# Early results fetched one slice ahead, final transposes in the small banks, and weight sums on VectorE, in a macaron FFN block

## The chip, the cores and the metric

The kernel runs on one core of a Trainium2 chip. Its time is that of one launch, in device microseconds (us). TensorE has two clock levels, 1.2 and 2.4 GHz; the profile gives the granted clock as a share of the upper one.

## The reference

One layer of a streaming encoder on x of 1024 tokens by 1024 features, all in fp32: a half-step FFN, a mixing stage (a chunkwise matrix-memory branch and a spatial gating branch), a second half-step FFN and a final norm.

```python
def swiglu(x, w_in, w_out):
    gate, up = jnp.split(x @ w_in, 2, axis=-1)
    return (jax.nn.silu(gate) * up) @ w_out
...
        x = x + 0.5 * swiglu(rmsnorm(x, ffn1_norm_g[l]), ffn1_w_in[l], ffn1_w_out[l])
        xn = rmsnorm(x, mix_norm_g[l])
        proj = xn @ w_mix_in[l]
...
        x = x + merged @ w_mix_out[l]
        x = x + 0.5 * swiglu(rmsnorm(x, ffn2_norm_g[l]), ffn2_w_in[l], ffn2_w_out[l])
    return rmsnorm(x, final_norm_g)
```

The hidden width `D_FF` is 2816, which is 22 slices of 128 columns. Only the two FFNs and the final norm are touched here.

## The kernel before

**Numbers and products.** Every fp32 operand is split into a high part (a cast on ScalarE, engine name ACT) and a low part (a subtract on VectorE, DVE), both fp32r. A product takes three matmuls (high by high, high by low, low by high), so four contraction tiles are 12 matmuls of 128x512. `unit` makes such a pair of a weight tile into the pool `fw` of four buffers, `split` does it for activations.

**The input GEMM of an FFN** is done by a Strassen-like scheme over a 2x2 partition: gate and up columns by the halves of the contraction, and the two halves of the tokens. Of the seven products of a slice, two depend on the token half whose operand is there first. `first_products` makes them for all 22 slices at the start of the FFN and stores the two results per slice (a partial sum, and a silu) in DRAM, tiles `eb`. `group(f)` does the rest of slice f, in this order:

- four loads of raw weights into two tiles of the pool `raw` (four buffers; L284, issued by SyncE, SP), then the two early results `p1` (L329) and `sg1` (L331) from `eb` into temporaries `c`, on the same queue;
- ScalarE copies `p1` into a PSUM bank x (L333), which opens the accumulation there;
- GpSimd (POOL) makes three sums of weight tiles (`sums`, L303 to L305): s1 = a21 + a22, a21 = a11 - a21, a11 = s1 - a11. Since they work in place, each waits for the raw tiles of both halves;
- five products of 12 matmuls (L297): t2 into x, t1 into a bank b, t3 into y (y is a copy of x, L338), 22 into x, t4 into y. The operands of t1, t3 and 22 are sums; that of 22 is one more subtract on GpSimd, L348. VectorE adds and multiplies what comes out (L347, L351, L355, L356) and makes the operands of the output GEMM (L367 to L373, L196).

**The output GEMM.** Slices are worked in blocks of 4, 4, 4, 4, 2 and 4. Each of the first four blocks has its output GEMM in `down_fast`, 4 x 42 matmuls, whose weight sums (L303 to L305 with 128x256 operands) are made by VectorE already and whose results are added into DRAM by DMAs on GpSimd's queue. A block's output GEMM is written behind the first slice of the next block, so the slice that follows it is the second of that block (slices 5, 9, 13, 17). Block 5 (slices 16 and 17) uses `down` behind slice 18. The last block, slices 18 to 21, uses `last`: for each of 8 output tiles d, 12 matmuls (L444), an add of the residual on VectorE (L471), and in the second FFN `fin2`, which transposes the sum on TensorE (L1021), multiplies it by the norm's gain (L1024) and, when the row's statistic is there, scales it (L1038).

**Buffers and order.** PSUM has 8 banks; in both FFNs seven are `mm`, from which `bank("mm")` takes, and one is `ml`, from which `psm()` takes for statistics and small things. The temporaries `c` and `t512` share 11 buffers. The program is written by hand; a scheduler at build time then fixes the order on each engine, and each engine and each DMA queue works its own list strictly in that order.

Of the kernel before, what the change touches and what calls it, by code (L numbers as in the profile page):

```python
# [11 lines left out]
ALU = mybir.AluOpType  # L12
# [7 lines left out]
NF = DFF // P  # L20
# [14 lines left out]
def block_body(ctx, tc, x, ffn1_norm_g, ffn1_w_in, ffn1_w_out, mix_norm_g, w_mix_in, mlstm_conv_w,  # L35
               mlstm_conv_b, mlstm_b_igate, mlstm_b_fgate, mlstm_head_norm_g, sgu_norm_g, sgu_norm_b,
               sgu_w_s, sgu_b_s, w_mix_out, ffn2_norm_g, ffn2_w_in, ffn2_w_out, final_norm_g, out):
    nc = tc.nc
    V, A, PE, G = nc.vector, nc.scalar, nc.tensor, nc.gpsimd
    x = x[0]  # L40
    out = out[0]
# [8 lines left out]
    def open_psum(stack, n, **bufs):  # L50
        for tag, b in bufs.items():
            psum[tag] = stack.enter_context(
                tc.tile_pool(name=f"{tag}{n}", bufs=b, space=bass.MemoryType.PSUM, reuse_waits="tile"))

    def bank(tag):
        return psum[tag].tile([P, NH], F32, tag=tag, name=tag)

    f1 = ExitStack()
# [3 lines left out]
    def open_temps(stack, n, bufs):  # L62
        raws.append(stack.enter_context(tc.tile_pool(name=f"rawp{n}", bufs=3 if n == 2 else 4, reuse_waits="tile")))
        tps.append(stack.enter_context(tc.tile_pool(name=f"tp{n}", bufs=bufs, reuse_waits="tile")))

    open_temps(f1, 1, TMP)
    open_psum(f1, 1, mm=7, ml=1)

    def t512():
        return tps[-1].tile([P, NH], F32, tag="t512", name="t512")  # L70
# [1 line left out]
    def psm():  # L72
        return bank("ml")
# [42 lines left out]
    def pc(nm, i):  # L116
        return par[:, col[nm] + i:col[nm] + i + 1]
# [29 lines left out]
    def spread():  # L147
        if todo:
            todo.pop(0)()
# [115 lines left out]
    def evens(src):  # L265
        return src[:, :, 0, :], src[:, :, 1, :]

    class Ffn:
# [39 lines left out]
        def first_products(self, fs):  # L308
# [9 lines left out]
            for f, a, e in st:  # L318
# [2 lines left out]
                A.activation(out=e[:, 1, :], in_=a, func=AF.Silu)  # L321
                G.dma_start(out=self.eb[f][1], in_=e[:, 1, :])

        def group(self, f):
            r1, r2 = self.raw(f, 0, True), self.raw(f, 1, True)
            a11, a21 = evens(r1)
            a12, a22 = evens(r2)
            p1 = self.c512()
            nc.sync.dma_start(out=p1, in_=self.eb[f][0])  # L329
            sg1 = self.c512()  # L330
            nc.sync.dma_start(out=sg1, in_=self.eb[f][1])  # L331
            x = bank("mm")
            A.copy(out=x, in_=p1)  # L333
            s1 = self.sums(G, a11, a12, a21, a22, 4)
            w = self.unit(a11)
            self.prod(x, w, self.B["t2"], False, True)
            y = bank("mm")
            A.copy(out=y, in_=x)  # L338
            w = self.unit(s1)
            b = bank("mm")  # L340
            self.prod(b, w, self.B["t1"], True, True)
            p5 = self.c512()
            A.copy(out=p5, in_=b)
            w = self.unit(a21)
            self.prod(y, w, self.B["t3"], False, True)
            c22 = self.c512()
            V.tensor_tensor(out=c22, in0=y, in1=p5, op=ALU.add)  # L347
            G.tensor_tensor(out=a12, in0=a12, in1=a11, op=ALU.subtract)  # L348
            w = self.unit(a12)
            self.prod(x, w, self.B["22"], False, True)  # L350
            V.tensor_tensor(out=p5, in0=x, in1=p5, op=ALU.add)  # L351
            A.activation(out=p5, in_=p5, func=AF.Silu)
            w = self.unit(a22)
            self.prod(y, w, self.B["t4"], False, True)
            V.scalar_tensor_tensor(out=sg1, in0=y, scalar=0.5, in1=sg1, op0=ALU.mult, op1=ALU.mult)  # L355
            V.scalar_tensor_tensor(out=c22, in0=c22, scalar=0.5, in1=p5, op0=ALU.mult, op1=ALU.mult)  # L356
            u3 = sg1
            if f >= FAST:
                self.hs.append((self.part(self.hp, u3), self.part(bigp, c22)))
            elif f % 2 == 0:  # L360
                self.H["11"].append(self.part(self.hp, u3))
                self.odd = u3, c22
            else:
                h11, h12 = self.odd
                H = self.H
                H["21"].append(self.part(self.hp, u3))
                V.tensor_tensor(out=h11, in0=h12, in1=h11, op=ALU.subtract)  # L367
                H["t1"].append(self.part(bigp, h11))
                V.tensor_tensor(out=h12, in0=c22, in1=h12, op=ALU.subtract)
                H["t3"].append(self.part(bigp, h12))  # L370
                V.tensor_tensor(out=h11, in0=c22, in1=h11, op=ALU.subtract)
                H["t2"].append(self.part(bigp, h11))
                V.tensor_tensor(out=u3, in0=u3, in1=h11, op=ALU.subtract)  # L373
                H["22"].append(self.part(self.hp, c22))
                H["t4"].append(self.part(bigp, u3))
# [99 lines left out]

        def run(self, src, final, parts, hook):
            pend = None
            for bi, (f0, n) in enumerate(BLOCKS):
                hs = self.hs = []
                H = self.H = {k: [] for k in ("11", "21", "22", "t1", "t2", "t3", "t4")}  # L480
                for f in range(f0, f0 + n):
                    self.group(f)
                    if pend is not None:
                        pend()
                        pend = None
                    spread()
                if f0 < FAST:
                    pend = lambda f0=f0, H=H: self.down_fast(f0, H, src)
                elif bi < len(BLOCKS) - 1:
                    pend = lambda f0=f0, n=n, hs=hs: self.down(f0, n, hs, src)  # L490
                else:
                    self.last(f0, n, hs, src, final, parts, hook)
# [488 lines left out]
        xn2, bcs, st = mix(mx, xnm)  # L981

    with ExitStack() as f2:
        open_psum(f2, 3, mm=7, ml=1)
        open_temps(f2, 3, TMP)
        ffn2 = Ffn(f2, "2", ffn2_w_in[0], ffn2_w_out[0])
        ffn2.B["11"], ffn2.B["21"] = xn2[:4], xn2[4:]

        def get2(j, i, t):
            b = ffn2.c512()  # L990
            d = 4 * j + i
            if t == 0:
                G.dma_start(out=b, in_=xs_[1][d])
                return b
            G.dma_start(out=b, in_=xd[1][t][d])
            V.scalar_tensor_tensor(out=b, in0=b, scalar=pc("g2", d), in1=bcs[t], op0=ALU.mult, op1=ALU.mult)
            return b

        ffn2.first_products((0, 1))
        bcs.append(st.bcast())  # L1000
        for i in range(4):
            ffn2.first_products((2 * i + 2, 2 * i + 3))
            ffn2.operands(i, get2)
        for f in range(10, NF, 2):
            ffn2.first_products((f, f + 1))

        PARTS = (1, 2)
        sts = [[Stats(4 // p) for _ in range(p)] for p in PARTS]
        fgs = []
        ys = []  # L1010

        def fin2(h, d, part, xt):
            n = 4 // PARTS[h]
            if not fgs:
                fgs.append(bigp.tile([P, D], F32, tag="big", name="fg"))
                nc.sync.dma_start(out=fgs[0], in_=final_norm_g.partition_broadcast(P))
            fg = fgs[0]
            sts[h][part].add(xt)
            ps = bank("mm")
            for t in range(n):  # L1020
                PE.transpose(out=ps[:, t * P:(t + 1) * P], in_=xt[:, t * P:(t + 1) * P], identity=ident)  # L1021
            if d % 2 == 0:
                ys.append(bigp.tile([P, n, 2 * P], F32, tag="big", name="y"))
            V.tensor_tensor(out=ys[-1][:, :, (d % 2) * P:(d % 2 + 1) * P],  # L1024
                            in0=ps[:, 0:n * P].rearrange("p (t c) -> p t c", c=P),
                            in1=fg[:, None, d * P:(d + 1) * P].to_broadcast([P, n, P]), op=ALU.mult)
            if d < KT - 1:
                return
            r = sts[h][part].rstd()
            t0 = h * NH + part * n * P  # L1030
            ov = out[t0:t0 + n * P, :].rearrange("(t p) c -> p t c", p=P)
            for i in range(4):
                y = ys.pop(0)
                for t in range(n):
                    if t == n - 1:
                        A.activation(out=y[:, t, :], in_=y[:, t, :], func=AF.Copy, scale=r[:, t:t + 1])  # L1036
                    else:
                        V.tensor_scalar(out=y[:, t, :], in0=y[:, t, :], scalar1=r[:, t:t + 1], scalar2=None,  # L1038
                                        op0=ALU.mult)
                nc.sync.dma_start(out=ov[:, :, i * 2 * P:(i + 1) * 2 * P], in_=y)  # L1040

        ffn2.run(xd[1], fin2, PARTS, lambda t, xs: None)


# [25 lines left out]
```

## Time and profile before

| | before |
|---|---|
| median of 3 runs | 2380.12 us (2379.06 to 2381.86) |
| the profiled execution, its own time | 2376.19 us |
| its span in the trace | 2374.4 us |
| mean granted clock | 0.979 |
| TensorE busy | 2258.1 us, 95% |
| VectorE busy | 1453.2 us, 61% |
| ScalarE busy | 1120.8 us, 47% |
| GpSimd busy | 496.7 us, 21% |

The span runs from the first to the last record of one execution; its own time is 1.8 us more. Matmul is PE in the rows, weight load PEld. TensorE stands for some 5% of the span, and part of its busy time is at a clock below the upper level.

### The profile page before, as it was taken

Reading aid. Unit: us, or ns where it says so; the run is one execution under the profiler, and the core shown is the slowest. Engines: PE = TensorE matmul, PEld = TensorE weight load, DVE = VectorE, ACT = ScalarE, POOL = GpSimd, SP = SyncE. Lnnn points to the kernel's source line nnn. Section 1 sums busy time; section 2 is a strip of 40 time slices with the busy share of each in tenths; the row PEclk is TensorE's granted clock in tenths of the full one; section 3 lists DMA queues with packets and bytes.
Section 4 is the critical chain, followed back from the end, with each engine's and each line's share of the span. In section 5 each row is a group of like instructions: output and inputs, shape, how many; then the busy total and the mean of one; then the engine's idle time right before and its main releaser. Section 6 shows DMA issues by size and latency. Waiting matters only on the chain. (4 is left out here: it accounts for less than half of the span.)

```text
span 2374.4 us, 30679 instructions
## 1 busy us (share of the span) xinstructions
PE 2258.1 (95%) x10979; PEld 1881.8 (79%) x10979; DVE 1453.2 (61%) x2563; ACT 1120.8 (47%) x1924; POOL 496.7 (21%) x557
## 2 busy tenths in 40 slices
PE   7999999999899999999999999999999999999896
PEld 5888787777778988888889878887887787777675
DVE  6647676675366757656656666564647576765355
ACT  5545454444444356444445455453545454544432
POOL 3242433414520000000000000001241524324420
PEclk8999999999999999999999999999999999999999
DMA  8853655637753334233343433325762745646632
GB/s 271 252 179 98 142 117 132 133 89 138 155 186 109 88 85 135 83 89 89 115 129 93 134 113 93 92 83 178 247 190 89 151 108 132 129 120 133 147 110 89
DMA packets 331512, 311.51 MB, mean 131 GB/s; under 512 B 19160, under 2 KB 279896, under 8 KB 331360
## 3 DMA queue, kind: packets, MB, share of 16 engines
q1 hardware_dynamic: 292608, 217.20, 31.1%
q0 software_dynamic: 38752, 92.36, 17.8%
q8 instruction: 86, 1.41, 0.2%
q14 instruction: 66, 0.54, 0.1%
HBM read 223.48 MB, written 86.02 MB: 130 GB/s over the span
## 5 line engine op out<-in xcount | busy, mean ns | idle before, releaser
L297 PE MATMUL mm<-b,fw 128*128 128x512 f32 x2640 | 626.4, 399 | 56.7 <-ACT mm L333 55.7
L297 PEld LDWEIGHTS mm<-b,fw 128*128 128x128 f32 x2640 | 508.1, 193 | 174.6 <-ACT mm L333 64.0
L291 DVE TENSOR_TENSOR fw<-raw,fw 128x512 fp32r<-128x512 f32 (+1 forms) x472 | 316.0, 676 | 396.4 <-ACT fw L290 394.9
L162 PE MATMUL mm<-xn,w 128*128 128x512 f32 x2304 | 546.6, 391 | 0.0
L162 PEld LDWEIGHTS mm<-xn,w 128*128 128x128 f32 x2304 | 427.0, 188 | 82.8
L297 PE MATMUL mm<-h,fw 128*128 128x512 f32 x1344 | 313.6, 393 | 5.8 <-ACT fw L290 3.1
L297 PEld LDWEIGHTS mm<-h,fw 128*128 128x128 f32 x1344 | 248.5, 188 | 69.6 <-ACT fw L290 8.2
L290 ACT CAST fw<-raw 128x512 fp32r<-128x512 f32 (+1 forms) x472 | 247.8, 526 | 101.5 <-PE mm L297 71.6
L138 DVE TENSOR_TENSOR w<-raw,w 128x1024 fp32r<-128x1024 f32 (+3 forms) x160 | 178.6, 1117 | 163.6 <-ACT w L137 163.2
L297 PE MATMUL mm<-xn,fw 128*128 128x512 f32 x1056 | 247.4, 396 | 3.6 <-ACT xn L195 2.1
L297 PEld LDWEIGHTS mm<-xn,fw 128*128 128x128 f32 x1056 | 200.5, 191 | 49.4 <-ACT xn L195 3.7
L137 ACT CAST w<-raw 128x1024 fp32r<-128x1024 f32 (+3 forms) x160 | 153.8, 963 | 178.7 <-PE mm L162 86.2
L176 PE MATMUL mm<-w,xn 128*128 128x256 f32 x1344 | 163.9, 282 | 0.0
L176 PEld LDWEIGHTS mm<-w,xn 128*128 128x128 f32 x1344 | 161.8, 189 | 1.4 <-issue 0.5
L256 POOL DMA_DIRECT2D xs<-t x16 | 8.6, 541 | 642.0 <-DVE t L253 641.3
L195 ACT CAST h<-c 128x512 fp32r<-128x512 f32 x136 | 82.2, 621 | 69.1 <-DVE c L355 26.3
L303 POOL TENSOR_TENSOR s<-raw 128x512 f32<-128x512 f32 x44 | 59.4, 1351 | 205.7 <-DMA raw<-in_ffn_w_in_dram 190.3
L444 PE MATMUL mm<-h,wl 128*128 128x512 f32 (+1 forms) x480 | 97.3, 356 | 0.3 <-DVE h L196 0.2
L196 DVE TENSOR_TENSOR h<-c,h 128x512 fp32r<-128x512 f32 x136 | 91.1, 689 | 5.9 <-ACT h L195 4.8
L409 POOL DMA_DIRECT2D xd<-c x32 | 28.0, 874 | 309.6 <-ACT fw L290 273.0
L444 PEld LDWEIGHTS mm<-h,wl 128*128 128x128 f32 x480 | 78.4, 192 | 12.5 <-DVE h L196 0.7
L162 PE MATMUL po<-mh,w 128*128 128x512 f32 x384 | 87.5, 389 | 0.0
(258 smaller groups left out, 2607.6 us busy)
## 6 DMA issues: line engine op xcount, KB each, us to landing
raw<-in_ffn_w_in_dram SPq DMA_DIRECT2D x264, 256.0 KB, 3.4
raw<-in_w_mix_in_dram SPq DMA_DIRECT2D x96, 512.0 KB, 3.8
xd<-c POOLq DMA_DIRECT2D x160, 256.0 KB, 5.2
eb<-early POOLq DMA_DIRECT2D x88, 256.0 KB, 2.8
c<-eb SPq DMA_DIRECT2D x88, 256.0 KB, 4.3
raw<-in_ffn_w_out_dram SPq DMA_DIRECT2D x72, 256.0 KB, 3.0
raw<-in_w_mix_in_dram SPq DMA_DIRECT2D x32, 384.0 KB, 3.4
xl<-xd POOLq DMA_DIRECT2D x32, 256.0 KB, 4.4
```

Of the source, the lines that this page charges most:

```text
L137: A.copy(out=w[:, 0, 0:n, :], in_=raw[:, 0:n, :])
L138: V.tensor_tensor(out=w[:, 1, 0:n, :], in0=raw[:, 0:n, :], in1=w[:, 0, 0:n, :].bitcast(F32), op=ALU.subtract)
L162: PE.matmul(out=banks[j], lhsT=w[:, a, i, j * P:(j + 1) * P], rhs=act[k][:, b, ts], start=(k == first and pi == 0), stop=(k == last and pi ...
L176: PE.matmul(out=o, lhsT=act[k][:, b, t * P:(t + 1) * P], rhs=w[:, a, i, :], start=(t % 2 == 0 and k == 0 and pi == 0), stop=(t % 2 == 1 an ...
L195: A.copy(out=dst[:, 0, :], in_=src)
L196: V.tensor_tensor(out=dst[:, 1, :], in0=src, in1=dst[:, 0, :].bitcast(F32), op=ALU.subtract)
L290: A.copy(out=w[:, 0], in_=src)
L291: V.tensor_tensor(out=w[:, 1], in0=src, in1=w[:, 0].bitcast(F32), op=ALU.subtract)
L297: PE.matmul(out=bank, lhsT=w[:, x, i, :], rhs=t[:, y, :], start=(start and i == 0 and pi == 0), stop=(stop and i == len(b) - 1 and pi == 2 ...
L303: G.tensor_tensor(out=s1, in0=a21, in1=a22, op=ALU.add)
L409: G.dma_start(out=acc[0][d], in_=c11, accum_op=ALU.add)
L444: PE.matmul(out=o, lhsT=w[:, x, i, :], rhs=hs[i][:, y, ts], start=(i == 0 and pi == 0), stop=(i == n - 1 and pi == 2))
```

## The change

Three edits. `group(f)` no longer loads its own early results; a new `fetch(f + 1)` is written right behind slice f's raw loads, and `fetch(0)` at the start of `run`. In both FFNs the PSUM split goes from 7 and 1 to 6 and 2, and the final transposes take `psm()`. The three sums of `group` and the subtract of a12 go from GpSimd to VectorE: 4 operations for each of 22 slices in two FFNs, 176 in all.

```diff
-    open_psum(f1, 1, mm=7, ml=1)
+    open_psum(f1, 1, mm=6, ml=2)
...
+        def fetch(self, f):
+            self.ahead = self.c512(), self.c512()
+            for t, src in zip(self.ahead, self.eb[f]):
+                nc.sync.dma_start(out=t, in_=src)
+
         def group(self, f):
             r1, r2 = self.raw(f, 0, True), self.raw(f, 1, True)
             a11, a21 = evens(r1)
             a12, a22 = evens(r2)
-            p1 = self.c512()
-            nc.sync.dma_start(out=p1, in_=self.eb[f][0])
-            sg1 = self.c512()
-            nc.sync.dma_start(out=sg1, in_=self.eb[f][1])
+            p1, sg1 = self.ahead
+            if f + 1 < NF:
+                self.fetch(f + 1)
             x = bank("mm")
             A.copy(out=x, in_=p1)
-            s1 = self.sums(G, a11, a12, a21, a22, 4)
+            s1 = self.sums(V, a11, a12, a21, a22, 4)
...
-            G.tensor_tensor(out=a12, in0=a12, in1=a11, op=ALU.subtract)
+            V.tensor_tensor(out=a12, in0=a12, in1=a11, op=ALU.subtract)
...
             pend = None
+            self.fetch(0)
...
-        open_psum(f2, 3, mm=7, ml=1)
+        open_psum(f2, 3, mm=6, ml=2)
...
-            ps = bank("mm")
+            ps = psm()
```

Lines of `group` from L333 on stand four lines lower afterwards (L337, L342, L351, L352 for the subtract, L355, L359, L360), L444 is L448, L1021 is L1026. How the built lists differ is seen at three places.

**SyncE's queue, first FFN, around slice 9**, the first slice behind an output GEMM. `eb080` and `eb081` are slice 8's early results, `eb090` and `eb091` slice 9's, `eb0100` and `eb0101` slice 10's; `raw_3328` and `raw_3331` (before) are slice 9's weights, `raw_3453` and `raw_3456` slice 10's. Before:

```order
L386 DMA raw_3058<-in_ffn1_w_out_dram 128x4x128 x2
L329 DMA c_2868<-eb080_197 128x512
L331 DMA c_2870<-eb081_198 128x512
L386 DMA raw_3148<-in_ffn1_w_out_dram 128x4x128 x2
L386 DMA raw_3238<-in_ffn1_w_out_dram 128x4x128 x2
L284 DMA raw_3328<-in_ffn1_w_in_dram 128x4x128 x2
L284 DMA raw_3331<-in_ffn1_w_in_dram 128x4x128 x2
L284 DMA raw_3453<-in_ffn1_w_in_dram 128x4x128 x2
L284 DMA raw_3456<-in_ffn1_w_in_dram 128x4x128 x2
L329 DMA c_3334<-eb090_199 128x512
L331 DMA c_3336<-eb091_200 128x512
```

After:

```order
L390 DMA raw_3062<-in_ffn1_w_out_dram 128x4x128 x2
L327 DMA c_2872<-eb090_199 128x512
L327 DMA c_2873<-eb091_200 128x512
L390 DMA raw_3152<-in_ffn1_w_out_dram 128x4x128 x2
L390 DMA raw_3242<-in_ffn1_w_out_dram 128x4x128 x2
L284 DMA raw_3332<-in_ffn1_w_in_dram 128x4x128 x2
L284 DMA raw_3335<-in_ffn1_w_in_dram 128x4x128 x2
L284 DMA raw_3457<-in_ffn1_w_in_dram 128x4x128 x2
L284 DMA raw_3460<-in_ffn1_w_in_dram 128x4x128 x2
L327 DMA c_3338<-eb0100_201 128x512
L327 DMA c_3339<-eb0101_202 128x512
```

The places in the list are the same; what stands at each is the pair of the next slice. Slice 9's pair is now ahead of two tiles of `w_out` and of four raw tiles, its own and slice 10's.

**VectorE, same place.** `c_3377` and `c_3394` (before) are slice 9's p5 and c22, `raw_3453` and `s_3465` slice 10's weights and sum. Before, from slice 9's last weight units on:

```order
L291 TENSOR_TENSOR fw_3414<-raw_3331,fw_3414 128x512
L291 TENSOR_TENSOR fw_3469<-raw_3453,fw_3469 128x512
L347 TENSOR_TENSOR c_3394<-mm_3359,c_3377 128x512
L291 TENSOR_TENSOR fw_3486<-s_3465,fw_3486 128x512
L351 TENSOR_TENSOR c_3377<-mm_3338,c_3377 128x512
L291 TENSOR_TENSOR fw_3504<-raw_3453,fw_3504 128x512
```

After, where `raw_3457` and `raw_3460` are slice 10's weights, `raw_3563` and `raw_3566` slice 11's, `c_3381` and `c_3398` slice 9's p5 and c22:

```order
L291 TENSOR_TENSOR fw_3418<-raw_3335,fw_3418 128x512
L291 TENSOR_TENSOR fw_3473<-raw_3457,fw_3473 128x512
L303 TENSOR_TENSOR s_3575<-raw_3563,raw_3566 128x512
L351 TENSOR_TENSOR c_3398<-mm_3363,c_3381 128x512
L291 TENSOR_TENSOR fw_3490<-s_3469,fw_3490 128x512
L304 TENSOR_TENSOR raw_3563<-raw_3563 128x4x128
L305 TENSOR_TENSOR raw_3563<-s_3575,raw_3563 128x4x128
L355 TENSOR_TENSOR c_3381<-mm_3342,c_3381 128x512
L291 TENSOR_TENSOR fw_3508<-raw_3457,fw_3508 128x512
L352 TENSOR_TENSOR raw_3566<-raw_3566,raw_3563 128x4x128
```

The first sum of slice 11, which needs slice 11's raw tiles, stands ahead of slice 9's c22 and of slice 10's second weight unit, and three more new operations stand between the rest.

**TensorE, the end of the program**, the first output tiles of the last output GEMM. Before:

```order
L444 MATMUL mm<-h,wl 128x512 x12
L1021 MATMUL mm<-ident,xl 128x128 x4
L444 MATMUL mm<-h,wl 128x512 x12
L1021 MATMUL mm<-ident,xl 128x128 x4
L444 MATMUL mm<-h,wl 128x512 x12
```

After:

```order
L448 MATMUL mm<-h,wl 128x512 x19
L1026 MATMUL ml<-ident,xl 128x128 x4
L448 MATMUL mm<-h,wl 128x512 x9
L1026 MATMUL ml<-ident,xl 128x128 x4
L448 MATMUL mm<-h,wl 128x512 x12
```

The transposes of a tile stood directly behind its own 12 matmuls; now 7 of the next tile's 12 matmuls stand between at first, 4 from the second tile on, and 8 and more where the tiles are 256 wide.

## Rows read from the trace of the kernel before

**Rows 1.** The page's busy times and its header.
```profile
span 2374.4 us, 30679 instructions
...
PE 2258.1 (95%) x10979; PEld 1881.8 (79%) x10979; DVE 1453.2 (61%) x2563; ACT 1120.8 (47%) x1924; POOL 496.7 (21%) x557
```

**Rows 2.** TensorE's waits: total us, times, longest.
```profile
PE mm L297 <- ACT mm L333: 55.7, 18, 9.6
PE mm L1021 <- DVE xl L471: 16.8, 23, 3.2
```

**Rows 3.** What line L333 waits for, and L329's issue to landing.
```profile
  DMA c<-eb: 115.3, 40
...
DMA to landing us min/median/max: 3.0/4.2/8.4
```

**Rows 4.** Timeline around slice 9: start us, us; in brackets idle before, releaser.
```profile
359.74 0.44 SPq L329 DMA_DIRECT2D c<-eb  x1
...
363.00 12.22 SPq L284 DMA_DIRECT2D raw<-in_ffn_w_in_dram  x4
...
366.44 0.59 ACT L333 COPY mm<-c 128x512 f32<-128x512 f32 x1 [2.41 <-DMA c<-eb]
...
367.08 3.36 PE L297 MATMUL mm<-b,fw 128*128 128x512 f32 x7 [4.19 <-ACT mm L333]
...
375.32 0.45 SPq L329 DMA_DIRECT2D c<-eb  x1
```

**Rows 5.** Windows after the ten longest L333 waits: us, PE busy, clock, DMA.
```profile
265.03:275.03 10.00, 10.00 (x37) 0.83 0.67 154
...
2243.99:2253.99 10.00, 10.00 (x33) 0.73 0.59 117
sum 100.00, PE 99.99; mean PE 10.00
```

**Rows 6.** Chain that ended last, the first tile pair of the tail.
```profile
2290.42 0.75 PE mm L444 x2
2291.19 0.70 DVE xl L471
...
2291.94 0.66 PE mm L1021 x4
```

**Rows 7.** Two slices without a wait: PE, PEld, DVE, ACT, POOL, clock.
```profile
397.60:424.90 27.30, 27.30 (x120) 22.63 (x121) 23.11 (x38) 13.86 (x26) 4.14 (x3) 1.00 0.33 97
```

**Rows 8.** Lines of GpSimd's sums and VectorE's like operations: busy, mean ns, idle before.
```profile
L305 POOL TENSOR_TENSOR raw<-s,raw 128x512 f32<-128x512 f32 x44 | 74.2, 1687 | 1.7
L348 POOL TENSOR_TENSOR raw<-raw 128x512 f32<-128x512 f32 x44 | 67.3, 1530 | 3.1
L304 POOL TENSOR_TENSOR raw<-raw 128x512 f32<-128x512 f32 x44 | 64.2, 1459 | 2.0
L303 POOL TENSOR_TENSOR s<-raw 128x512 f32<-128x512 f32 x44 | 59.4, 1351 | 205.7 <-DMA raw<-in_ffn_w_in_dram 190.3 <-DVE c L347 13.9 <-DVE fw L291 1.4
...
L356 DVE SCALAR_TENSOR_TENSOR c<-c 128x512 f32<-128x512 f32 x44 | 51.9, 1180 | 5.3 <-ACT c L352 5.0
...
L367 DVE TENSOR_TENSOR c<-c 128x512 f32<-128x512 f32 x16 | 11.1, 692 | 0.6
```

**Rows 9.** VectorE's timeline, two operations back to back.
```profile
388.67 0.68 DVE L373 TENSOR_TENSOR c<-c 128x512 f32<-128x512 f32 x1
389.27 0.68 DVE L196 TENSOR_TENSOR h<-c,h 128x512 fp32r<-128x512 f32 x1
```

**Rows 10.** Timeline: slice 9's c22 and slice 11's first sum.
```profile
377.92 0.69 DVE L347 TENSOR_TENSOR c<-mm,c 128x512 f32<-128x512 f32 x1 [0.89 <-PE mm L297]
...
378.98 1.43 POOL L303 TENSOR_TENSOR s<-raw 128x512 f32<-128x512 f32 x1 [9.31 <-DMA raw<-in_ffn_w_in_dram]
```

**Rows 11.** Timeline: slice 20's first sum, slice 19's first product.
```profile
626.45 1.25 POOL L303 TENSOR_TENSOR s<-raw 128x512 f32<-128x512 f32 x1 [6.78 <-DMA raw<-in_ffn_w_in_dram]
...
631.07 17.26 PE L297 MATMUL mm<-b,fw 128*128 128x512 f32 x67 [6.99 <-ACT mm L333]
```

## Prediction

> **What bounds the kernel now.** I read the busy times first: TensorE is at work for 2258.1 of 2374.4 us [rows 1]. The reader is to see that no engine beside it is near the span, so the time is matmuls, the time TensorE stands, and the time it works at the lower clock. The second view is therefore the list of TensorE's waits, since only a wait there is sure to be on the path. One entry leads it: 55.7 us in 18 waits for the copy at L333, which puts slice f's early result into its bank; next come 16.8 us in 23 waits of the final transposes for the add at L471 [rows 2]. The third view is what L333 itself waits for: DMAs out of `eb`, 115.3 us in 40 waits, although a load lands some 4.2 us after its issue [rows 3]. So the load is issued late, and the timeline says why: slice 9's pair stands on SyncE's queue behind slice 10's raw loads (the order shows it), is issued at 359.74, its copy runs at 366.44, and TensorE starts at 367.08 after 4.19 us of nothing; slice 11's raw loads then hold the queue for 12.22 us, and slice 10's pair goes at 375.32 [rows 4].
>
> The fourth view is windows of 10 us behind the ten longest of these waits. They show what a wait costs beyond itself: the granted clock there is 0.83, 0.75, 0.77, 0.83, 0.81, 0.69, 0.85, 0.83, 0.74 and 0.73 [rows 5], though TensorE is busy throughout. Behind waits under 2 us it stays at 1.00, as in the two slices of [rows 7]. A window at clock c does 10c us of full-speed work, so the loss is 10 times the sum of (1 - c): 10 x (10 - 7.83) = 21.7 us.
>
> **Early results a slice ahead.** The two orders of SyncE's queue show that places stay and contents move by one slice. Slice 9's pair takes the place of slice 8's, some 52 us earlier (four output tiles of 42 matmuls at 0.2275 us, the 27.30/120 of [rows 7], and a slice of 13.65); slice 10's pair goes at 359.74 where slice 9's went, lands by 366.4, and is wanted when slice 9 is done: TensorE would start slice 9 at 367.08 - 4.19 = 362.9, and end it at 376.5. There are 10 us to spare. No DMA is added: 88 pairs' halves before, 88 after. The loads ahead on the queue take a `c` buffer each, two of eleven, which then are out of use for a slice longer; a load that waited for a buffer would hold the raw loads behind it. The buffers they reuse come from temporaries of a slice or an output tile earlier, so I cost that at nothing; its cover is the same 10 us, and if it is gone the raw loads are late by the rest. **Gain: 55.7 + 21.7 = 77.4 us.** The low end is 55.7, if something else lowers the clock there. What is late next at these places is the weight unit, and I come to it below.
>
> **Final transposes in the small banks.** TensorE's order at the end shows what decides: before, a tile's four transposes stand directly behind its own 12 matmuls and wait for the residual's add, as in the chain: matmuls end at 2291.17, the add takes 0.70, the transposes start at 2291.94 [rows 6]. Afterwards some of the next tile's matmuls stand between, 4 at the least with 512 columns (0.91 us at 0.2275) and 8 or more with 256. That covers an add of 0.70 and the way to it. **Gain: 16.8 us**; the last tile keeps its wait, under a microsecond. With one bank for transposes instead of several, the multiply at L1024 would hold the next transposes; there are two, and a tile's 12 matmuls lie between two uses. The input GEMM has six banks for seven. A slice takes three, x, y and b, so two slices in flight fit. I cost it at nothing: the first writer of a bank waits, at the worst, for a read of the bank three places earlier. If that cover is gone, each slice pays one copy of 0.59 [rows 4], 44 x 0.59 = 26 us.
>
> **Sums on VectorE.** 176 operations go off GpSimd, where they take 59.4 + 64.2 + 74.2 + 67.3 = 265 us [rows 8], off the path: no TensorE wait names them. On VectorE the like operation is L367, fp32 from two SBUF tiles, 692 ns [rows 8]; back to back such operations start 0.60 us apart [rows 9]. In two steady slices VectorE ran 38 records in a window of 27.30 us [rows 7]; by the program a pair has 29 operations (10 in an even slice, 19 in an odd one), which become 37. At 0.605 that is 22.4 us in 27.3, so VectorE keeps up, with 4.9 us a pair to spare, and I cost the work itself at nothing. It gets a little back: L356 takes 1180 ns beside GpSimd's L348 and should fall towards 700 when GpSimd is quiet.
>
> By the Trainium skill, page "VectorE: DVE Perf Modes", section "The DRAIN you can't avoid", the next operation does not start until the pipe is empty, unless it is one that is not held back. Taken as it stands each would cost its whole 0.69, and a pair 37 x 0.69 = 25.5 us of 27.3; [rows 9] show a start 0.60 after the last one, so the trace does not agree for such neighbours, and the sum goes by the row.
>
> The same skill's page "Perfetto Trace Analysis", section "Optimizing Scalar/DVE Operations", says that GpSimd and VectorE share a read port, so that moving work between the two might not help. By that alone the 176 operations would bring VectorE 1.35 to 1.69 us each; [rows 8] have 692 ns for L367, and nothing of GpSimd's adds is left to share with.
>
> What does cost is the wait that comes along. The order puts slice f+2's first sum ahead of slice f's c22 and of the second unit of slice f+1 on VectorE. That sum needs f+2's raw tiles, and GpSimd has waited for them until now, 190.3 us in 34 waits [rows 8], where it hurt nobody. In steady slices VectorE comes to it when c22 could run, at 377.92, and the tiles are there for the sum at 378.98 [rows 10]: 1.1 us in which c22 and the units behind it stand. Later units have some 1 to 2 us of lead by my count of 37 x 0.605, less at the end of a block. I take 0.5 us of TensorE for each of the eight blocks with a fast output GEMM, 4 us. Slice 19 is worse: slice 20's tiles are there at 626.45 [rows 11], and slice 19, freed of its 6.99 us wait, would start at 631.07 - 6.99 = 624.1 and want its t1 unit one product later, at 626.8; three sums and a subtract behind the landing it is ready at 626.45 + 4 x 0.605 = 628.9. That is 2 us in each FFN, 4 us. **Loss: 8 us**; its bounds are nothing, and 1.5 us in each of 32 slices with the clock's loss on top, about 60.
>
> **Sum.** 2376.2 (the profiled execution's own time) - 77.4 - 16.8 + 8 = 2290.0. That execution was 3.9 us under the median of the runs shown; as the terms are absolute, the median should be 2380.1 - 86.2 = 2293.9. I predict 2294.
>
> **The rivals.**
> - Forecast, chance 0.70: some 86 us less, 2280 to 2308.
> - VectorE's waits for raw tiles come through to TensorE, 0.15. For it speaks that its list is strictly in order and the new sums wait for DMAs; against it that the tiles land about when c22 is wanted. At 1.5 us in each of the 32 slices of the fast blocks, 48 us, and a lower clock behind a few of them, some 10, it is 2294 - 8 + 58 = 2344. Still faster.
> - VectorE becomes the bound, 0.07, the one on the other side. Its place is the pair of slices; it decides when waits at the head of its list exceed the 1.7 us (37 operations at L367's 0.692 are 25.6) to 4.9 us (at 0.605) a pair that are over. If each of two sums a pair waits as long as slice 9 did for its raw loads, 6.1 us (half of the 12.22 us issue of [rows 4]), a pair takes 25.6 + 12.2 = 37.8 instead of 27.3. Over 16 pairs that is 168 us, and 2380 - 94 + 168 = 2454. Against it: raw loads are issued when buffers come free, so a slower TensorE has them in time, and the loop does not feed itself.
> - The fetch does not do what it says, 0.05: its place on the queue is again behind loads that wait, and the pair is as late as before. Then the transposes alone count: 2380 - 17 = 2363. The two lists speak against it.
> - The sums cost what the rest gains, 0.03: no change.
>
> **How the numbers follow.** The first case alone goes from 2280 (no loss on VectorE and a few short waits gone too) to 2308 (twice the loss, half the clock's gain kept). For 8 in 10 the range reaches part of the way to the second: 2274 to 2335. A measurement of this kernel can tell about 0.2%, 4.8 us, from no change. Faster: 0.70 + 0.15 + 0.05 less a little of each = 0.88; same 0.04; slower 0.08.
>
> **What would show it.** Right: TensorE's waits for the copy of the early result (L337) under 5 us; the clock near 1.00 behind each output GEMM; the waits of the transposes (L1026) under 2 us; the four sums gone from GpSimd, on VectorE at about 0.69 us with waits of 1 to 2 us for raw tiles ahead of the first. Wrong: TensorE waits named after the weight subtract (L291) or cast (L290) of tens of microseconds, or for bank releases in the copies (L342). The prediction fails if VectorE's waits reach TensorE in every slice, or if the clock falls at other places for them.

## The result

The changed kernel takes 2304.06 us (median of 4 runs, 2298.88 to 2308.23) where the kernel before, run beside it, takes 2380.99 (2379.06 to 2382.28): a ratio of 0.9676, 95% interval 0.9655 to 0.9698. That is 76.9 us less; 86 were forecast, and 2304 lies in the stated range. The profiled execution of the changed kernel took 2305.36 us.

The header and the busy times of its page, which answer to [rows 1]:

```profile
span 2303.6 us, 30578 instructions
...
PE 2231.6 (97%) x10979; PEld 1872.1 (81%) x10979; DVE 1466.3 (64%) x2739; ACT 1119.3 (49%) x1924; POOL 252.7 (11%) x381
```

176 operations have left GpSimd and are on VectorE, whose busy time rose by only 13 us. TensorE's waits in the changed kernel, answering to [rows 2] (total us, times, longest):

```profile
PE mm L297 <- DVE fw L291: 17.8, 2, 11.0
PE mm L297 <- DVE c L351: 17.1, 9, 2.8
...
PE ml L1026 <- DVE xl L475: 0.5, 1, 0.5
```

Neither wait that the change aimed at is left: no entry names the copy of the early result (L337), and the transposes wait 0.5 us in all. Two new entries of 34.9 us stand in their place, where the prediction had 8. Both come from the sums' waits, which now stand on VectorE:

```profile
DVE s L303 <- DMA raw<-in_ffn_w_in_dram: 101.1, 39, 17.6
```

The larger price is at slice 19 of each FFN. The changed kernel's timeline there (start, us, idle before and its releaser in brackets):

```profile
605.82 0.69 DVE L303 TENSOR_TENSOR s<-raw 128x512 f32<-128x512 f32 x1 [17.62 <-DMA raw<-in_ffn_w_in_dram]
606.54 0.69 DVE L304 TENSOR_TENSOR raw<-raw 128x512 f32<-128x512 f32 x1
...
608.62 3.57 PE L297 MATMUL mm<-b,fw 128*128 128x512 f32 x8 [10.99 <-DVE fw L291]
```

VectorE stands 17.62 us before slice 20's first sum, with slice 19's t1 unit behind it, and TensorE stands for 10.99. The smaller price is at the first slice behind a fast output GEMM, here slice 5, whose c22 stands behind the sum of slice 7:

```profile
264.26 0.69 DVE L291 TENSOR_TENSOR fw<-raw,fw 128x512 fp32r<-128x512 f32 x1 [2.03 <-ACT fw L290]
269.86 0.69 DVE L303 TENSOR_TENSOR s<-raw 128x512 f32<-128x512 f32 x1 [4.90 <-DMA raw<-in_ffn_w_in_dram]
270.47 0.68 DVE L351 TENSOR_TENSOR c<-mm,c 128x512 f32<-128x512 f32 x1
...
271.30 3.89 PE L297 MATMUL mm<-b,fw 128*128 128x512 f32 x16 [2.77 <-DVE c L351]
```

This is what [rows 10] had at 1.1 us: the sum waits 4.90, slice 5's c22 stands behind it, and t4, which writes the bank that c22 reads, starts 2.77 us late. Six of the nine waits named L351 are of this kind, 15.1 of the 17.1 us.

To see where the whole difference went, I cut each trace at TensorE's own records into stretches: the eight fast output GEMMs (168 matmuls each), the eight stretches of slices that follow them, slices 19 to 21 in each FFN (180 matmuls), and the second FFN's last output GEMM with its transposes. Windows of the changed kernel over one of each (start and end, length, then busy time of PE, PEld, DVE, ACT and POOL with the number of operations, the granted clock, the DMA engines' busy share and GB/s):

```profile
218.81:257.65 38.84, 38.84 (x170) 31.39 (x169) 25.40 (x53) 22.81 (x50) 12.40 (x15) 1.00 0.76 140
257.65:315.08 57.43, 54.66 (x242) 44.97 (x241) 43.34 (x74) 26.52 (x48) 1.45 (x2) 1.00 0.47 126
...
594.45:649.47 55.02, 42.86 (x181) 34.71 (x181) 28.65 (x45) 20.72 (x37) 5.88 (x10) 0.91 0.52 141
...
2237.90:2294.30 56.40, 55.84 (x365) 48.45 (x363) 39.13 (x98) 17.26 (x37) 4.36 (x8) 1.00 0.30 98
```

and of the kernel before:

```profile
221.44:261.15 39.71, 39.08 (x169) 30.88 (x167) 27.30 (x49) 22.44 (x49) 17.56 (x19) 1.00 0.75 135
261.15:323.23 62.08, 56.88 (x242) 46.31 (x242) 40.40 (x62) 27.12 (x49) 18.39 (x14) 0.97 0.43 118
624.08:673.94 49.86, 42.87 (x182) 35.39 (x182) 24.94 (x35) 21.39 (x38) 20.47 (x22) 0.93 0.69 171
2287.45:2365.18 77.73, 60.61 (x365) 49.68 (x363) 40.42 (x98) 17.53 (x37) 4.25 (x8) 0.98 0.22 73
```

The sums over all such stretches, for every kernel of this study (us, in the profiled execution: an output GEMM from its first to its last TensorE record, slices from the end of the output GEMM before them to the start of the next one, so that a wait at their start is in; the median of the runs in the last column):

| kernel | 8 fast output GEMMs | 8 stretches of slices behind them | slices 19 to 21, first and second FFN | last output GEMM, second FFN | median |
|---|---|---|---|---|---|
| before | 319.4 | 439.5 | 49.7, 53.0 | 77.7 | 2380.99 |
| changed | 310.7 | 399.4 | 54.9, 50.6 | 56.4 | 2304.06 |
| fetch alone | 319.3 | 388.9 | 41.0, 40.6 | 77.5 | 2300.31 |
| banks alone | 318.4 | 441.4 | 52.6, 53.4 | 56.4 | 2356.88 |
| sums alone | 310.7 | 437.3 | 62.6, 60.0 | 78.6 | 2380.69 |
| fetch and banks | 319.5 | 385.9 | 45.9, 41.2 | 56.5 | 2276.78 |
| changed, sums behind the last unit | 310.8 | 379.5 | 49.2, 47.5 | 56.4 | 2277.43 |
| the same for slice 20 only | 310.8 | 398.5 | 48.8, 49.5 | 56.4 | 2296.33 |
| changed, 32 transfers left out | 310.8 | 402.3 | 40.6, 40.6 | 56.4 | 2283.00 |
| changed, sums behind c22 | 310.5 | 394.1 | 47.6, 48.0 | 56.4 | 2294.24 |
| sums behind c22, last block's on GpSimd | 310.5 | 394.2 | 41.4, 46.0 | 56.4 | 2283.82 |
| sums behind c22, 8 idle adds a slice | 334.6 | 443.5 | 49.2, 49.5 | 64.8 | 2408.53 |
| sums behind the last unit, last block's on GpSimd | 310.7 | 379.5 | 41.4, 42.2 | 56.4 | 2266.20 |

Without a wait the slices' column would be 379.5 (the value at which it stands in two runs) and the next one some 40.6 for each FFN. From the kernel before to the changed one the four columns of stretches give -8.7, -40.1, +2.8 and -21.3, together -67.3 of the 70.8 us between the spans.

### The profile page after: what moved, and what is told of

The parts are those of the page before. It is cut to its first block, busy times and chain, and to the rows that moved or that the text cites. A ratio compares the mean times of both kernels' runs of the same rounds, so it can differ in the third digit from the quotient of the medians.

```text
span 2303.6 us, 30578 instructions
## 1 busy us (share of the span) xinstructions
PE 2231.6 (97%) x10979; PEld 1872.1 (81%) x10979; DVE 1466.3 (64%) x2739; ACT 1119.3 (49%) x1924; POOL 252.7 (11%) x381
## 5 line engine op out<-in xcount | busy, mean ns | idle before, releaser
L297 PE MATMUL mm<-b,fw 128*128 128x512 f32 x2640 | 610.5, 393 | 34.9 <-DVE fw L291 17.8
L297 PEld LDWEIGHTS mm<-b,fw 128*128 128x128 f32 x2640 | 499.9, 190 | 143.6 <-issue 19.1
L291 DVE TENSOR_TENSOR fw<-raw,fw 128x512 fp32r<-128x512 f32 (+1 forms) x472 | 267.2, 570 | 260.1 <-ACT fw L290 258.7
L290 ACT CAST fw<-raw 128x512 fp32r<-128x512 f32 (+1 forms) x472 | 248.1, 526 | 148.5 <-PE mm L297 121.4
L297 PE MATMUL mm<-h,fw 128*128 128x512 f32 x1344 | 310.7, 391 | 0.0
L303 DVE TENSOR_TENSOR s<-raw 128x512 f32<-128x512 f32 (+1 forms) x76 | 44.0, 579 | 107.7 <-DMA raw<-in_ffn_w_in_dram 101.1
L195 ACT CAST h<-c 128x512 fp32r<-128x512 f32 x136 | 80.9, 620 | 51.6 <-DVE c L359 23.2
L448 PE MATMUL mm<-h,wl 128*128 128x512 f32 (+1 forms) x480 | 95.9, 353 | 0.0
L448 PEld LDWEIGHTS mm<-h,wl 128*128 128x128 f32 x480 | 77.3, 189 | 12.0 <-ACT h L195 0.5
L162 PEld LDWEIGHTS po<-mh,w 128*128 128x128 f32 x384 | 71.9, 188 | 14.9
```

The costliest lines, as they stand in the source:

```text
L162: PE.matmul(out=banks[j], lhsT=w[:, a, i, j * P:(j + 1) * P], rhs=act[k][:, b, ts], start=(k == first and pi == 0), stop=(k == last and pi ...
L195: A.copy(out=dst[:, 0, :], in_=src)
L290: A.copy(out=w[:, 0], in_=src)
L291: V.tensor_tensor(out=w[:, 1], in0=src, in1=w[:, 0].bitcast(F32), op=ALU.subtract)
L297: PE.matmul(out=bank, lhsT=w[:, x, i, :], rhs=t[:, y, :], start=(start and i == 0 and pi == 0), stop=(stop and i == len(b) - 1 and pi == 2 ...
L303: G.tensor_tensor(out=s1, in0=a21, in1=a22, op=ALU.add)
```

## Experiments: one edit at a time

**Without the third edit.** From the changed kernel:

```diff
-            s1 = self.sums(V, a11, a12, a21, a22, 4)
+            s1 = self.sums(G, a11, a12, a21, a22, 4)
...
-            V.tensor_tensor(out=a12, in0=a12, in1=a11, op=ALU.subtract)
+            G.tensor_tensor(out=a12, in0=a12, in1=a11, op=ALU.subtract)
```

> The whole change without its third edit: early results a slice ahead and transposes in the small banks, but the weight sums stay on GpSimd. Theory of the prediction (sums on VectorE cost 8 us): the time is about 8 us under the changed kernel's 2304, some 2296. Theory from the trace after (the sums' order on VectorE makes the 34.9 us of new waits behind L291 and L351, with some 7 us of lower clock, and gives back 9 us in the fast output GEMM): 2304 - 35 - 7 + 9 = 2271, no TensorE wait of over 2 us at slices 6, 10, 14 and 19, and the fast output GEMM's 168 matmuls at 39.7 us again instead of 38.84. Against both: if GpSimd's late sums now hold TensorE up in the same places, it is 2304 or more.

Measured: 2276.78 us against 2379.29 of before on the same chip, ratio 0.9575 (0.9549 to 0.9601). So the third edit, put on top of the other two, costs some 25 us: 24 by the two ratios (0.0101 of 2380), 24.7 by the spans of the profiled executions (2303.6 and 2278.9). The stretches show three parts: the slices behind the output GEMMs are 13.5 us shorter without it, slices 19 to 21 together 18.4 us, and the fast output GEMMs 8.7 us longer. The second theory holds, within 6 us (the slices that it numbers 6, 10 and 14 are 5, 9 and 13): at the slices behind the output GEMMs no wait over 1.4 us is left, but one of 3.4 us named L351 is in slice 19 of the first FFN.

**The transposes' edit alone.** The change's three bank lines on the kernel before.

> The transposes' edit alone (6 and 2 banks, final transposes in the small ones) on the kernel before. Prediction: 16.8 us gone, 2364. From the trace after, where the last output GEMM of the second FFN took 56.2 us for 77.6: 21 us gone, 2360. If six banks hold up the input GEMM, some 26 us come back and it is 2381 or more.

Measured: 2356.88, ratio 0.9910 (0.9879 to 0.9940), 22.4 us less. The interval holds both 2364 and 2360; the trace tells them apart, since the last output GEMM accounts for 21.3 us. Six banks instead of seven cost nothing that shows: the stretches of slices are 441.4 for 439.5.

**The sums alone.** The change's two lines from GpSimd to VectorE on the kernel before.

> The weight sums on VectorE alone, on the kernel before. Prediction: 8 us slower, 2389, since the early results still come late. Theory from the trace after: the fast output GEMMs gain 9 us (38.8 for 39.8 us each), the waits behind L303 fall partly into the waits for the early results, so the cost is 35 less what is hidden: 2372 to 2405, with GpSimd's accumulating transfers of the block of two closer together and slice 20's raw tiles landing later after that block's output GEMM began than the 24.2 us of the kernel before.

Measured: 2380.69, ratio 1.0007 (0.9991 to 1.0022): no difference, and the 8 us that the prediction would add (0.34%) lie outside the interval. It is a balance, not an absence: the fast output GEMMs gain 8.7 us, the slices behind them 2.2, and slices 19 to 21 lose 19.8. (That sums to 9 us more; the spans of the two profiled executions differ by 7.4, the medians by 1.4.) The new waits of the changed kernel are hidden here by the late early results, as the second theory had it, and slice 20's raw tiles land 31.6 us after the block's output GEMM began, for 24.2 before. At slice 19 the early result itself comes later still, in this kernel's timeline of TensorE:

```profile
636.03 4.21 PE L297 MATMUL mm<-b,fw 128*128 128x512 f32 x9 [19.45 <-ACT mm L333]
```

**The fetch alone.** `fetch` and its calls on the kernel before.

> The fetch a slice ahead alone, on the kernel before. Prediction: 77.4 us gone, 2304 (the eight units of loss belong to the sums). Theory from the trace after: the waits for L333 and their clock are gone here too, about 77, and no new wait behind L351: 2304 or a few us less; rival, that the sums on GpSimd are late next and take 20 to 30 us of it back: 2325 to 2335.

Measured: 2300.31, ratio 0.9674 (0.9646 to 0.9702), 79.0 us less: the fetch alone does what the whole change does. Fetch (79.0) and banks (22.4) add up to 101.4; together they gave 102.5.

## Experiments: what the sums cost, and why

**Order on VectorE.** The first sum of a slice is queued behind the last weight unit of the slice before it; nothing waits for that unit to finish. `self.done` is the subtract of the unit of a22.

```diff
+            with self.after_units(f):
+                s1 = self.sums(V, a11, a12, a21, a22, 4)
...
+        def after_units(self, f):
+            return tc.issue_after(self.done) if f else nullcontext()
```

> The changed kernel with one thing more: on VectorE the first sum of a slice is ordered behind the last weight unit of the slice before it (issue order only), so that no unit and no c22 of an earlier slice stands behind a sum that waits for raw tiles. Theory that this order is the price of the third edit: the waits behind L351 (17.1 us) and L291 (17.8 us) go, their lower clock too, the fast output GEMM stays at 38.8 us per block, and the time is 2304 - 35 - 7 = 2262, some 9 us under fetch and banks alone with 2277 less the 5 us of that one's slice 19. Rival, that VectorE has too much work for the stretch: it stays within 10 us of 2304, with the waits under other names.

> The same for slice 20 alone in each FFN. Theory of the order: the two waits of slice 19 (11.0 and 6.8 us) and the clock behind them go, most of the 23.6 us by which slices 19 to 21 are over their 41.0 each, and the nine waits behind L351 stay: 2304 - 20 = 2284. Rival, that slice 19 stands for the transfers themselves: slice 20 then waits for its raw tiles instead and the time stays at 2304 less a few us.

Measured: 2277.43 (ratio 0.9584, 0.9561 to 0.9607) for all slices, 2296.33 (0.9658, 0.9636 to 0.9681) for slice 20 alone. In the first the stretches behind the output GEMMs are at 379.5, without a wait in any of them, and the fast output GEMMs keep their 310.8: the six waits behind L351 at these places come from the order and nothing else, 20 us with the clock behind them. The rival, too much work for VectorE, is out. By the ratios it took 22 us off, not 42, because slice 19 was cured in part only. Its wait has another name in that run (the line is c22's there):

```profile
PE mm L297 <- DVE c L355: 10.4, 2, 5.4
```

Slice 19's units now come in time, but its c22 still stands behind slice 20's sum, and the raw tiles of that one land late. The second of the two runs says the same: 6.1 and 1.1 us off the two stretches, not the 20 expected; its time is nearer the rival's, and its interval overlaps the changed kernel's.

**The transfers of the block of two.** In the block before slice 19, `down` sends 16 accumulating transfers from GpSimd's queue, 256 KB each. Here they are left out in both FFNs, and with them the contribution of slices 16 and 17 to the result.

```diff
-                        G.dma_start(out=acc[t][d + j], in_=xt, accum_op=ALU.add)
```

> The changed kernel without the 16 accumulating transfers of the block of two slices in each FFN; the contribution of slices 16 and 17 to the result is left out. Theory that these transfers, no longer held up by sums on GpSimd's queue, take the bandwidth from slice 20's raw tiles: these land within 4 us of their issue for 15 to 20, the waits of slice 19 fall from 11.0 and 6.8 us to under 2, and the time is 2304 - 20 = 2284 or less. Rival, that the raw tiles are issued too late whatever the traffic: the waits stay over 5 us.

Measured: 2283.00, ratio 0.9601 (0.9579 to 0.9623). Slices 19 to 21 take 40.6 us in both FFNs, no wait at all, although VectorE's order is that of the changed kernel. So slice 19's price needs these transfers; that it needs the sums on VectorE as well is seen in the run of the fetch alone (41.0 and 40.6). The raw loads of slice 20 go at the same distance from the start of the block's output GEMM in both kernels (the last pair 12.5 us behind it), so they were not issued too late, as the rival has it. The DMA issues of the three kernels over the same stretch (16 accumulating transfers and the raw loads beside them; KB, median us from issue to landing), of before:

```profile
xd<-c POOLq DMA_DIRECT2D x16, 256.0 KB, 6.1
raw<-in_ffn_w_in_dram SPq DMA_DIRECT2D x8, 256.0 KB, 5.2
```

of the changed kernel:

```profile
xd<-c POOLq DMA_DIRECT2D x16, 256.0 KB, 8.5
raw<-in_ffn_w_in_dram SPq DMA_DIRECT2D x5, 256.0 KB, 11.4
```

and of the run without them:

```profile
raw<-in_ffn_w_in_dram SPq DMA_DIRECT2D x8, 256.0 KB, 3.0
```

Why they collide more now is on GpSimd's timeline. Before:

```profile
607.94 1.56 POOL L303 TENSOR_TENSOR s<-raw 128x512 f32<-128x512 f32 x1
609.58 1.36 POOL L304 TENSOR_TENSOR raw<-raw 128x512 f32<-128x512 f32 x1
610.89 0.87 POOL L437 DMA_DIRECT2D xd<-c  x1
...
614.60 5.06 POOL L437 DMA_DIRECT2D xd<-c  x5
```

After:

```profile
583.18 0.86 POOL L441 DMA_DIRECT2D xd<-c  x1 [0.55 <-ACT c L440]
...
594.22 0.87 POOL L441 DMA_DIRECT2D xd<-c  x1 [0.66 <-ACT c L440]
595.37 0.86 POOL L441 DMA_DIRECT2D xd<-c  x1 [0.28 <-ACT c L440]
```

Before, the sums of slices 19 and 20 stood between the transfers on the same list; slice 20's waited 6.78 us for its raw tiles [rows 11], and the last six transfers waited behind it: none was issued between 616.84 and 627.65. The DMA engines were busy all the same, but with ten transfers instead of 16 ahead of or beside the raw tiles, and these were complete 24.2 us after the block's output GEMM began. With GpSimd empty, each transfer goes as soon as its data is there, a new one every 1.3 us on average (16 from 575.5 to 595.4), and slice 20's tiles, issued at 580 to 586, are complete at 605.8 only, when the last transfer lands, 33.3 us after that output GEMM began.

**c22 first.** As the order run, with `self.done` set at c22's add instead of the last unit.

> The changed kernel with the first sum of a slice ordered on VectorE behind the c22 of the slice before it (issue order only), not behind its last weight unit as in the order run, where c22 of slice 19 still stood behind slice 20's sum and cost 5.4 and 5.0 us. Theory of the order: those two waits and the 5 us of lower clock behind them go as well: 2277 - 10 - 5 = 2262, slices 19 to 21 near 42 us. Rival, that slice 20's raw tiles, landing late among the accumulating transfers, then hold slice 20 itself: slices 19 to 21 stay at 45 or more and the time at 2270 to 2277.

> The same, but the weight sums of the last block (slices 18 to 21) stay on GpSimd, whose queue they share with the accumulating transfers of the block of two. If holding those transfers back is worth something beside the right order on VectorE, slice 20's raw tiles land earlier than in the run with c22 first and the time is 3 to 10 us under it; if the order was all, it is the same within 3 us.

Measured: 2294.24 (0.9645, 0.9630 to 0.9659) with c22 first, 2283.82 (0.9605, 0.9588 to 0.9622) with the last block's sums on GpSimd besides. My theory of the order fell here: c22 first is some 15 us worse than the last unit first (0.0061 of 2380). In the blocks the sums now come so late that the next slice's own first units are late (eight waits for L291 and eight for the copy L346, up to 0.9 us each, in slices 4, 8, 12 and 16; the stretches behind the output GEMMs take 394.1 for 379.5). And slice 19 did not gain, since its c22 waits for something else, on ScalarE:

```profile
610.09 0.59 ACT L340 COPY mm<-c 128x512 f32<-128x512 f32 x1 [10.08 <-DMA c<-eb]
610.61 0.58 ACT L351 COPY c<-mm 128x512 f32<-128x512 f32 x1
```

The copy of slice 20's early result, late in the same traffic, stands ahead of slice 19's p5. With the last block's sums on GpSimd, slices 19 to 21 fall to 41.4 and 46.0, and the time by 10.4 us: the upper end of the 3 to 10 expected.

**Idle adds on GpSimd.** As the run with c22 first, and 8 adds of 128x256 a slice into a tile that nobody reads:

```diff
+            scr = self.sp_.tile([P, 2, P], F32, tag="scr", name="scr", bufs=1)
+            for _ in range(8):
+                G.tensor_tensor(out=scr, in0=s1[:, :2], in1=s1[:, 2:], op=ALU.add)
```

> The run with c22 first and, for each slice, 8 adds of 128x256 on GpSimd into a scratch tile that nobody reads, behind the slice's first sum: GpSimd works at the old places again, and VectorE keeps the real sums. Theory that a busy GpSimd lengthens VectorE's operations: the fast output GEMM goes from 38.8 back to 39.5 to 40 us a block and VectorE's 128x256 subtract L291 from 422 to some 560 ns; the time is 7 to 15 us over the run without them. Rival, that the fast output GEMM gained because its neighbours' sums no longer came late: it stays at 38.8.

Measured: 2408.53, ratio 1.0137 (1.0097 to 1.0177), 114 us over the run without them where 7 to 15 were expected; only the direction held. The adds take GpSimd 367 us, more than the 265 of [rows 8], and lengthen VectorE's operations that read two SBUF tiles. The same sum, without the adds and with them:

```profile
L305 DVE TENSOR_TENSOR raw<-s,raw 128x512 f32<-128x512 f32 x44 | 30.3, 689 | 0.9
```

```profile
L305 DVE TENSOR_TENSOR raw<-s,raw 128x512 f32<-128x512 f32 x44 | 56.7, 1288 | 0.9
```

The 128x256 subtract L291 went from 423 to 543 ns (560 were expected), while c22's add, which reads PSUM and one SBUF tile, took 692 ns without and 691 with them. The fast output GEMM went to 41.4 us or more, past the 39.5 to 40 expected; the rival's 38.8 is out. That a busy GpSimd makes VectorE's operations with two SBUF inputs longer is shown; that this alone makes the 0.9 to 1.1 us of the fast output GEMM is not shown by this run, because the adds also stand between the accumulating transfers on GpSimd's list.

**The parts that paid.** The last unit's order for slices up to 17, sums of slices 18 to 21 on GpSimd.

> The order run (first sum behind the last weight unit of the slice before) for slices 0 to 17, with the weight sums of the last block on GpSimd as in the run before. The parts seen singly should add: slices behind output GEMMs at 54.6 us, the fast output GEMM at 38.8, slices 19 to 21 at 41.8 to 46.4 for 49.5 and 47.9 in the order run: 2277 - 1.5 to 7.7 in each FFN, 2262 to 2274, the fastest so far, and under fetch and banks alone (2277). If it stays at 2277, the last block's price is not in its sums.

Measured: 2266.20, ratio 0.9532 (0.9508 to 0.9556), the fastest kernel here: by the ratios 34 us under the changed one and 10 under fetch and banks alone (whose interval, 0.9549 to 0.9601, overlaps it at the edge). Its windows over the first three stretches:

```profile
218.88:257.67 38.79, 38.79 (x170) 31.39 (x169) 25.49 (x53) 22.81 (x50) 12.36 (x15) 1.00 0.78 140
257.51:312.07 54.56, 54.56 (x242) 45.22 (x241) 44.70 (x74) 26.74 (x48) 1.62 (x2) 1.00 0.50 133
585.73:627.50 41.77, 41.23 (x182) 33.88 (x181) 24.63 (x35) 21.10 (x37) 19.91 (x22) 1.00 0.71 195
```

## Why the prediction was right, and where it was not

**Early results a slice ahead: right.** 77.4 us were forecast, the fetch alone gave 79.0. In the changed kernel L337 waits for its DMA four times for 40 before, and no entry of TensorE's waits names it. The clock term is part of it: behind the old waits the stretches are at 1.00 in the run with fetch and banks. The two extra `c` buffers cost nothing that shows. One reading of the prediction does not carry over, that the clock stays at 1.00 behind waits under 2 us: in the 10 us behind the changed kernel's six waits for L351 at slices 5, 9 and 13 the granted clock was 1.00 behind 2.25 to 2.80 us in four cases, and 0.83, a mix of the two levels, behind 1.99 and 2.51.

**Final transposes: right, a little small.** 16.8 was forecast, 22.4 measured alone. The list of waits held only the time in which TensorE stood; the two windows of the last output GEMM differ by 21.3 us, of which 16.6 are idle time by their span less busy time (17.1 and 0.6) and 4.8 are busy time: a period of one tile went from 4.19 us (chain of before) to 3.27, more than the 0.70 of the add. The granted clock of that window rose from 0.98 to 1.00 too; the rest of the 4.8 is not explained by these runs. The banks' price of 26 us, had the cover been gone, was not due.

**Sums on VectorE: the work is free, the waits are not.** VectorE kept up, as forecast. In the 54.56 us of the fastest kernel's second window above it is busy for 44.70 and TensorE never stands, so the rival in which VectorE becomes the bound did not come. (The prediction's 29 operations a pair leave out nine of the coming output GEMM that are among the 38 records of [rows 7]; its 4.9 us to spare were fewer there, without harm.) The step that failed is the size of the loss, 8 us: it is some 25, made of 13.5 and 18.4 us of new waits, with the clock behind them, and 8.7 us given back (23.2 of the 24.7 between the spans).

- The 4 us for the eight blocks should have been 13.5. I took the landing of slice f+2's tiles from [rows 10] and called it steady, but it is a stretch in which TensorE had just stood for 4.19 us and the traffic of the output GEMM had run off meanwhile: slice 11's last two raw loads, issued at 374.29 and 374.71, landed in 2.9 and 4.1 us. With the wait gone the loads go out into that traffic: slice 7's four, issued from 257.70 to 262.69 in the changed kernel, landed in 6.9 to 10.1. The DMA engines are busy there from the last accumulating transfers on until the tiles land (windows: length, PE busy, clock, DMA share, GB/s):

```profile
255.00:260.00 5.00, 5.00 (x23) 1.00 1.01 232
260.00:265.00 5.00, 5.00 (x24) 1.00 1.10 218
265.00:270.00 5.00, 3.53 (x16) 1.00 0.92 274
270.00:275.00 5.00, 3.70 (x16) 1.00 0.01 3
```

- The 4 us for slice 19 should have been 18.4, for the same reason and one more. I kept the landing at 626.45 of [rows 11], 2.4 us behind slice 19's freed start, and it came 11.5 us behind it (605.8 and 594.3). The prediction costed the 265 us that leave GpSimd at nothing, as work that no TensorE wait names. But GpSimd's list also issues the accumulating transfers, and its sums, by waiting for raw tiles, had held those transfers back.

- What was not forecast at all is the gain in the fast output GEMMs, 8.7 us: it comes with the sums whenever they leave GpSimd (310.5 to 310.8 in all eight runs that have them off it there, 318.4 to 319.5 in the four with them on it). I had said that L356 would fall towards 700, and it did, with its neighbours in the fast output GEMM, but gave that no price. The changed kernel's rows, and behind them that of L414 in the kernel before, where it is L410:

```profile
L360 DVE SCALAR_TENSOR_TENSOR c<-c 128x512 f32<-128x512 f32 x44 | 30.3, 688 | 5.8 <-ACT c L356 5.0
...
L414 DVE TENSOR_TENSOR raw<-raw 128x256 f32<-128x256 f32 x32 | 13.5, 423 | 0.8
```

```profile
L410 DVE TENSOR_TENSOR raw<-raw 128x256 f32<-128x256 f32 x32 | 26.8, 838 | 1.1
```

TensorE's rows of the eight fast output GEMMs, before and in the changed kernel, say how it got there:

```profile
L297 PE MATMUL mm<-h,fw 128*128 128x512 f32 x1344 | 313.6, 393 | 5.8 <-ACT fw L290 3.1 <-DVE c L414 1.9 <-DVE fw L291 0.8
```

```profile
L297 PE MATMUL mm<-h,fw 128*128 128x512 f32 x1344 | 310.7, 391 | 0.0
```

Of the 8.7 us, 5.8 are TensorE's waits for weight units (L290, L291) and for VectorE's add (L414 before), which are all gone, and 2.9 are busy time. The Trainium skill, page "SBUF — State Buffer", section "SBUF: two separate sides", describes this: a VectorE operation with two SBUF inputs and a GpSimd operation that reads SBUF lock each other out of a shared pair of ports for a whole instruction. The rows agree (838 to 423, 1180 to 688, and 689 to 1288 when idle adds are put in). That the fast output GEMM's gain comes from there alone stays argued: no run here takes GpSimd's adds away without changing what else its list does.

The forecast total was near because two misses were opposed: the gains came out 7 us larger than forecast (101.4 alone for 94.2), the loss some 17 larger, and 86 + 7 - 17 is 76. The rival in which waits for raw tiles come through to TensorE named the right mechanism; its price was a little over half of the 58 us given there (31.9).

## What to carry to other kernels

A wait that is taken away was also a pause for everything else: before you reuse a landing time or a slack from a stretch, ask whether the stall you remove was what made it. Work that goes from one in-order engine to another takes its waits along, so count what is queued behind each, and ask also what the old queue will now issue sooner. Where such work is wanted, an explicit place in the order (here behind the last unit of the slice before) was worth 22 us by the ratios, the neighbouring choice 7.

## What the runs showed of the hardware

- A chain of 16 accumulating transfers kept the DMA engines busy for some 30 us (share 0.91 to 1.13 from 575 to 600 in the changed kernel, 0.71 to 605), and ordinary loads issued beside it took 11.4 us at the median, where they take 3.0 without it; of one, issued at 585.45, the landing is not recorded, but the sum that waits for it starts 20.4 us later.
- VectorE's 128x512 operations of two SBUF inputs took 684 to 693 ns on average with GpSimd quiet and up to 1288 beside its adds, while an add with one input in PSUM kept its time (692 without them, 691 with them). With 265 us of adds off GpSimd each fast output GEMM on TensorE is 1.1 us shorter.
- The three chained sums start 0.72 and 0.73 us apart (605.82, 606.54, 607.27), not at the 0.60 of [rows 9].
